# A batched transposed product in float32: the first batch of a loaded ahead of the first pair of b, and the last wait moved from SyncE to GpSimd

## Chip, cores, metric

One core of one Trainium2 chip. The metric is the time of one execution in device microseconds, as a median of several runs. The span that a profile gives for the same execution is some 1.8 us shorter.

## The reference

```python
batch, m, k, n = 16, 512, 512, 512
a: float32 [batch, k, m];  b: float32 [batch, n, k]

def reference(a, b):
    return np.matmul(a.transpose(0, 2, 1), b.transpose(0, 2, 1)).astype(np.float32)
```

Each batch reads 1 MB of a and 1 MB of b and writes 1 MB: 50.33 MB in all.

## The kernel before

The kernel turns all of b before its products, so b's path is long: load, cast to bfloat16 (VectorE), transpose (TensorE), copy out of PSUM (VectorE), product. The path of a is load, cast (ScalarE), product. Batches of b come in pairs of 2 MB, in rows of 16 KB per partition; batches of a in transfers of 1 MB with rows of 8 KB. There are 4 buffers for a, 3 for pairs of b, 5 for pairs of outputs. SyncE issues all loads and the last stores, ScalarE the first five stores.

```python
def run_sp(sp):
    for i in range(B):
        for p in ([0] if i == 0 else [(i + 1) // 2] if i % 2 and i + 1 < B else []):
            if p >= PAIRS:
                sp.wait_ge(turned, p - PAIRS + 1)
            sp.dma_start(b_sb[p % PAIRS][:], b_v[p]).then_inc(b_in[p % PAIRS], 16)
        s, use = i % LOADS, i // LOADS
        if use:
            sp.wait_ge(summed, MO * (i - LOADS) + 1)
        if i % 2 == 0 and i // 2 >= OUTS:
            sp.wait_ge(o_out[i // 2 % OUTS], 16 * (i // 2 // OUTS))
        sp.dma_start(a_sb[s][:], a_v[i]).then_inc(a_in[s], 16)
    # ... stores of pairs 5 and 6 ...
    sp.wait_ge(summed, MO * (B - 1) + 1)
    sp.wait_ge(half_go, 1)
    store(sp, H - 1, slice(0, 1))        # last pair, first batch
    sp.wait_ge(last_go, 3)
    store(sp, H - 1, slice(1, 2))        # the last store
    sp.reg_mov(all_stored, 16 * STORED)

def run_act(act):
    cast_a(act, 0)
    for i in range(B - 1):
        cast_a(act, i + 1)
        copy_out(act, i, slice(2, 4), oa_go)
        # ... store of a pair, three batches behind ...
    act.drain().then_inc(half_go, 1)
    copy_out(act, B - 1, 2, last_go)
    copy_out(act, B - 1, 3, last_go)

# ... casts, copies and turns on VectorE, products on TensorE ...

nc.sync.wait_ge(stored, nc.sync.snap(all_stored))    # behind the section
```

Of the kernel before, what the change touches and what calls it, by code (L numbers as in the profile page):

```python
# [11 lines left out]
def kernel(  # L12
# [6 lines left out]
    nc = tc.nc  # L19
# [15 lines left out]
    a_v = a.rearrange("b (ki ko) m -> b ki ko m", ko=KO)  # L35
# [9 lines left out]
    STORED = H - (H - OUTS) + 1  # L45

    stored = tc.alloc_semaphore("stored")

    all_stored = nc.sync.alloc_register("all_stored")

    with tc.tile_critical():  # L51
        sb = lambda name, shape, dt: ctx.enter_context(nc.sbuf_tensor(name, shape, dt))
# [2 lines left out]
        a_sb = [sb(f"a_sb{s}", [P, KO, M], f32) for s in range(LOADS)]  # L55
# [12 lines left out]
        a_in = [sem(f"a_in{s}") for s in range(LOADS)]  # L68
# [14 lines left out]
        def store(eng, j, part=slice(0, 2)):  # L83

            eng.dma_start(
                out_v[2 * j + part.start:2 * j + part.stop].rearrange("b p mo n -> p b mo n"),
                o_sb[j % OUTS][:, part],
            ).then_inc(o_out[j % OUTS] if j + OUTS < H else stored, 16)

        def run_sp(sp):
            for i in range(B):

                for p in ([0] if i == 0 else [(i + 1) // 2] if i % 2 and i + 1 < B else []):
                    if p >= PAIRS:
# [5 lines that stand above are left out]
                if i % 2 == 0 and i // 2 >= OUTS:  # L101

                    sp.wait_ge(o_out[i // 2 % OUTS], 16 * (i // 2 // OUTS))
                sp.dma_start(a_sb[s][:], a_v[i]).then_inc(a_in[s], 16)

            for j in range(H - TAIL, H - 1):
                sp.wait_ge(summed, MO * (2 * j + 2) + 3)
                store(sp, j)

            sp.wait_ge(summed, MO * (B - 1) + 1)  # L110
            sp.wait_ge(half_go, 1)
            store(sp, H - 1, slice(0, 1))
            sp.wait_ge(last_go, 3)
            store(sp, H - 1, slice(1, 2))
            sp.reg_mov(all_stored, 16 * STORED)

        def run_pool(pool):
            pool.sem_inc(od_go, 1)
            pool.sem_inc(oa_go, 1)
            pool.memset(identity[:], 0.0).then_inc(id_go, 1)  # L120
            pool.wait_ge(id_go, 1)
            pool.affine_select(  # L122
                out=identity[:],
                in_=identity[:],
                compare_op=mybir.AluOpType.not_equal,
                fill=1.0,
                base=0,
                pattern=[[-1, P]],
                channel_multiplier=1,
            ).then_inc(id_go, 1)  # L130

        def cast_a(act, i):
            s = i % LOADS
            act.wait_ge(a_in[s], 16 * (i // LOADS + 1))
            act.copy(a_bf[i % 2][:], a_sb[s][:]).then_inc(ac_go, 1)  # L135
# [56 lines left out]
        def run_pe(pe):  # L192
# [41 lines left out]
            with pe.Fori(0, H) as _i:  # L234
# [6 lines left out]
                half(1, 1)  # L241

        run_sp(nc.sync)
        run_pool(nc.gpsimd)
        run_dve(nc.vector)
        run_act(nc.scalar)
        run_pe(nc.tensor)

    nc.sync.wait_ge(stored, nc.sync.snap(all_stored))  # L250

# [28 lines left out]
```

## Time and profile before

| | before |
|---|---|
| time | 124.8 us (124.68 to 124.91, 3 runs) |
| span | 123.0 us |
| bytes, mean rate | 50.33 MB, 409 GB/s |
| busiest compute engine | PE, 70% of the span |

The page's rows are the span in 40 slices, each digit a busy share in tenths. A stretch is read as: from:to, length, busy time of PE, PEld, DVE, ACT and POOL with counts, granted TensorE clock, DMA share, GB/s (PE is TensorE, PEld its weight loads, DVE VectorE, ACT ScalarE, POOL GpSimd, SP SyncE; a q behind the name is the engine's queue of instructions). A DMA share of 1 means that all 16 DMA engines have a packet in hand. "Landing" is when all of a transfer's semaphore counts have arrived. The lines themselves are in the prediction.

### The profile page before, as it was taken

To read this page: it belongs to the slowest core of one execution; us is meant where nothing else is said; L and a number is where in the kernel's file an instruction comes from. 1 tells how busy PE (TensorE), PEld (TensorE's weight loads), DVE (VectorE), ACT (ScalarE), POOL (GpSimd) and SP (SyncE) were. 2 spreads that over 40 slices of the span, in tenths; PEclk is the share of its full clock that TensorE was granted. 3 is DMA by queue.
4 is the path that set the end of the run, shared out by engine and by line. 5 is a ranking of instruction groups with operands and counts; after the bars stand their busy time and mean duration, and the time that the engine had idled before them with its cause. 6 is when DMAs were issued, how large, how long until landed. Compare 5 with 4: busy or idle time off the path is not lost. (4 is left out here: it accounts for less than half of the span.)

```text
span 123.0 us, 1086 instructions
## 1 busy us (share of the span) xinstructions
PE 86.1 (70%) x400; PEld 49.7 (40%) x400; DVE 56.4 (46%) x48; ACT 46.8 (38%) x34; POOL 0.7 (1%) x6
## 2 busy tenths in 40 slices
PE   0006497997999799779930799965992679979600
PEld 0006344642755464346410546442640526437300
DVE  0016368478295755917039107780719306171200
ACT  4003209537717903176300950329230490750300
POOL 2000000000000000000000000000000000000000
PEclk9999999999999999999995557999999558999995
DMA  4999999999999999999999999999999999999992
GB/s 91 394 400 458 400 424 456 429 394 456 426 397 448 434 376 432 426 440 440 416 421 429 458 408 418 429 426 437 453 397 432 426 426 426 429 426 426 429 424 115
DMA packets 5648, 50.33 MB, mean 409 GB/s; under 512 B 528, under 2 KB 528, under 8 KB 528
## 3 DMA queue, kind: packets, MB, share of 16 engines
q1 hardware_dynamic: 4288, 39.85, 77.2%
q10 hardware_dynamic: 1360, 10.49, 20.1%
HBM read 33.55 MB, written 16.78 MB: 409 GB/s over the span
## 5 line engine op out<-in xcount | busy, mean ns | idle before, releaser
L219 PE MATMUL o_ps<-bt_sb,a_bf 128*128 128x512 bf16 x256 | 65.1, 403 | 7.1 <-PEq L194 6.6
L135 ACT CAST a_bf<-a_sb 128x2048 bf16<-128x2048 f32 x16 | 30.4, 1900 | 40.8 <-DMA a_sb<-in_a_dram 40.8
L219 PEld LDWEIGHTS o_ps<-bt_sb,a_bf 128*128 128x128 bf16 x256 | 28.5, 115 | 37.5 <-issue 15.0
L205 PE MATMUL bt_ps<-identity,b_bf 128*128 128x128 f32 x144 | 24.3, 323 | 22.7 <-PEq L194 22.7
L144 DVE COPY o_sb<-o_ps 128x1024 f32<-128x1024 f32 x16 | 19.6, 1224 | 35.8 <-PE o_ps L219 35.8
L205 PEld LDWEIGHTS bt_ps<-identity,b_bf 128*128 128x128 f32 x144 | 22.2, 212 | 28.2 <-issue 27.2
L152 DVE CAST b_bf<-b_sb 128x2048 bf16<-128x2048 f32 x16 | 19.5, 1221 | 19.1 <-DMA b_sb<-in_b_dram 19.1
L144 ACT COPY o_sb<-o_ps 128x1024 f32<-128x1024 f32 (+1 forms) x17 | 16.4, 962 | 28.0 <-PE o_ps L219 28.0
L161 DVE COPY bt_sb<-bt_ps 128x1024 f32<-128x1024 f32 x16 | 19.5, 1216 | 3.1 <-PE bt_ps L205 3.1
L135 ACT ACT_TABLE_LOAD x1 | 1.3, 1283 | 0.9 <-SPq L51 0.9
L122 POOL TENSOR_SCALAR_AFFINE_SELECT identity<-identity 128x128 f32<-128x128 f32 x1 | 0.3, 294 | 0.2 <-POOL identity L120 0.2
L120 POOL MEMSET identity<- 128x128 f32 x1 | 0.2, 205 | 0.7 <-SPq L51 0.7
L265 POOL MEMSET const-bfloat16-1.0<- 128x1 bf16 x1 | 0.1, 102 | 0.0
L265 POOL MEMSET const-uint8-127<- 128x1 uint8 x1 | 0.1, 102 | 0.0
L265 POOL MEMSET const-float32-0.0<- 128x1 f32 x1 | 0.1, 99 | 0.2 <-issue 0.2
L265 POOL MEMSET const-float32-1.0<- 128x1 f32 x1 | 0.1, 99 | 0.0
## 6 DMA issues: line engine op xcount, KB each, us to landing
b_sb<-in_b_dram SPq DMA_DIRECT2D x8, 2048.0 KB, 20.4
a_sb<-in_a_dram SPq DMA_DIRECT2D x16, 1024.0 KB, 17.5
out_dram<-o_sb ACTq DMA_DIRECT2D x5, 2048.0 KB, 15.2
out_dram<-o_sb SPq DMA_DIRECT2D x2, 2048.0 KB, 13.6
out_dram<-o_sb SPq DMA_DIRECT2D x2, 1024.0 KB, 6.3
```

What stands on the lines that cost most here:

```text
L120: pool.memset(identity[:], 0.0).then_inc(id_go, 1)
L122: pool.affine_select(out=identity[:], in_=identity[:], compare_op=mybir.AluOpType.not_equal, fill=1.0, base=0, pattern=[[-1, P]], channel_ ...
L135: act.copy(a_bf[i % 2][:], a_sb[s][:]).then_inc(ac_go, 1)
L144: copy(o_sb[i // 2 % OUTS][:, i % 2, rm, :], o_ps[h][:, p, :]).then_inc(go, 1)
L152: dve.tensor_copy(b_bf[:, r, :], b_sb[p % PAIRS][:, r, :]).then_inc(bc_go, n)
L161: dve.tensor_copy(bt_sb[g][:].rearrange("p j (ni r) -> p j ni r", r=NR), bt_ps[:].rearrange("p j r (g ni) -> p g j ni r", g=2)[:, g],).the ...
L205: last = pe.transpose(bt_ps[:, j, r, :], w[:, r, j, :], identity[:])
L219: last = pe.matmul(o_ps[h][:, q, :], a_r[:, rk, 2 * h + q, :], bt_h[:, rk // 2, rk % 2, :], start=(rk == 0), stop=(rk == KO - 1),)
L265: nc = _bacc.Bacc("TRN2", target_bir_lowering=False, num_devices=1)
```

## The change

```diff
-    all_stored = nc.sync.alloc_register("all_stored")
+    all_stored = nc.gpsimd.alloc_register("all_stored")
@@ run_sp
             for i in range(B):
+                if i == 0:
+                    sp.dma_start(a_sb[0][:], a_v[0]).then_inc(a_in[0], 16)
@@
-                sp.dma_start(a_sb[s][:], a_v[i]).then_inc(a_in[s], 16)
+                if i:
+                    sp.dma_start(a_sb[s][:], a_v[i]).then_inc(a_in[s], 16)
@@
             store(sp, H - 1, slice(1, 2))
-            sp.reg_mov(all_stored, 16 * STORED)
@@ run_pool
+            pool.reg_mov(all_stored, 16 * STORED)
@@
-    nc.sync.wait_ge(stored, nc.sync.snap(all_stored))
+    nc.gpsimd.wait_ge(stored, nc.gpsimd.snap(all_stored))
```

## The prediction

> **What bounds the kernel now.** I began with the head of the page and its 40 slices, because a kernel of 16 matrix products can be bound by TensorE or by its traffic.
>
> ```profile
> span 123.0 us, 1086 instructions
> PE 86.1 (70%) x400; PEld 49.7 (40%) x400; DVE 56.4 (46%) x48; ACT 46.8 (38%) x34; POOL 0.7 (1%) x6
> ...
> PE   0006497997999799779930799965992679979600
> ...
> DMA  4999999999999999999999999999999999999992
> ...
> HBM read 33.55 MB, written 16.78 MB: 409 GB/s over the span
> ```
>
> The PE row has holes throughout; the DMA row has none between its first slice and its last. No compute engine is over 70% of the span. Next I cut the span into stretches, to see at which rate the transfers run and where they do not (columns: stretch, its length, busy time of PE, PEld, DVE, ACT and POOL with counts, granted TensorE clock, DMA share, GB/s).
>
> ```profile
> 2.00:3.00 1.00, 0.00 (x0) 0.00 (x0) 0.00 (x0) 0.18 (x1) 0.00 (x0) 1.00 1.06 213
> 3.00:4.00 1.00, 0.00 (x0) 0.00 (x0) 0.00 (x0) 0.00 (x0) 0.00 (x0) 1.00 0.71 262
> ...
> 30.00:60.00 30.00, 26.37 (x134) 15.57 (x135) 17.91 (x16) 15.60 (x12) 0.00 (x0) 1.00 1.01 425
> 60.00:90.00 30.00, 21.86 (x96) 12.18 (x93) 14.15 (x12) 10.96 (x8) 0.00 (x0) 0.83 1.01 430
> ...
> 120.00:121.00 1.00, 0.00 (x0) 0.00 (x0) 0.00 (x0) 0.00 (x0) 0.00 (x0) 0.50 0.70 295
> 121.00:122.00 1.00, 0.00 (x0) 0.00 (x0) 0.00 (x0) 0.00 (x0) 0.00 (x0) 0.50 0.04 16
> ```
>
> From 4 to about 120.5 us the rate stays near 427 GB/s, also where TensorE's clock is cut (mean 0.83 between 60 and 90 us). 50.33 MB at 427 GB/s are 117.9 us. The span is therefore: about 1.95 us until the first data packet starts, 1.2 us lost while the rate climbs (20 us into the span 7.18 MB have landed, which at full rate take 16.8 us, so the full-rate line starts at 3.2 us), 117.9 us of transfer, and the rest behind the last data. The chain of waits of the page covers only 5% of the span and stops at ScalarE's last copy, since the last transfer is not an instruction; I did not use it. SyncE's own waits and the issues show how deep the queue is:
>
> ```profile
> SPq L104 <- PE o_ps L219: 41.6, 10, 11.9
> SPq L103 <- DMA out_dram<-o_sb: 33.3, 3, 11.5
> ...
> SPq L276 <- DMA out_dram<-o_sb: 4.6, 1, 4.6
> ```
>
> SyncE waits for buffers for most of the run, yet the DMA engines do not go idle: the loads it has issued are far ahead. The loads' times from issue to landing show by how much:
>
> ```profile
> b_sb<-in_b_dram SPq DMA_DIRECT2D x8, 2048.0 KB, 20.4
> a_sb<-in_a_dram SPq DMA_DIRECT2D x16, 1024.0 KB, 17.5
> ```
>
> A 1 MB load takes 2.45 us at 427 GB/s; a median of 17.5 us means some 15 us of other transfers ahead of it. Over the whole run, behind the first two issues, the shortest is 13.7 us (the load of a issued at 27.2 us). So a stall of SyncE of under about 11 us would not show in the time.
>
> [...] the rate does not change when ScalarE's stores begin at 40 us. [...] The trace agrees for SyncE's first seven loads, which land in the order of issue at 8.8 (b), 11.2 (a), 16.1 (b), 18.6 (a), 21.1 (a), 26.0 (b) and 28.5 us (a). [...] the trace's semaphore records at the end step at 40 to 120 ns, which is the scale that the second part of the change can move.
>
> **The change part by part.** No byte is added or removed, and no compute instruction: VectorE, ScalarE and TensorE have the same instructions in the same order, SyncE one register move less, GpSimd one more. SyncE's first three issues become a, b, b instead of b, a, b; the fourth on is as before.
>
> Part one, start of the transfers. SyncE's first issue still starts at 0.95 us. The first packets start about 1.0 us after it, and take 0.7 to 1.9 us each instead of the 0.61 us that a 16 KB packet takes later. The ramp costs 1.2 us. With a first, the first packets are of 8 KB. If the slow phase is one of time, nothing changes; if each engine pays a delay on its first packet whatever its size, still nothing changes, since the delay is paid once. If it blocks two packets each instead of one, half a packet per engine is lost, 0.3 us. I take +0.05 us.
>
> Part one, compute. b's first pair lands 2.45 us later (8.8 to about 11.2 us), a's first batch earlier (11.2 to about 6.3). Before, b lands at 8.8 us, VectorE casts it in two halves (1.22 us each), TensorE transposes until 13.8, VectorE copies 1.23 us, and the first product starts at 15.55 us. ScalarE's cast of a, begun at 11.25 us and 1.90 us long, is over at 13.15, 2.4 us before it is needed. So the part hurries what had slack, and delays what had none: the first product starts at about 15.55 + 2.45 = 18.0 us. The following waits fold that in. The second pair of b still lands at 16.1 us, and after it VectorE's first gap before a load is only 0.39 us (at 26.0 us), so the lag persists there; but ScalarE waits 3.55 us for a load at 51.7 us and 8.16 us at 67.8 us, so it is gone by the middle. The loads waiting for a buffer are issued 2.45 us later at 16.7 and 17.0 us, in front of which 11.8 us of transfers are still queued (the last landing is 28.5). Nothing runs dry: 0 us.
>
> Part two, the end. The last store is issued at 116.54 us, its last packet ends at 121.45, its semaphore is full at 121.93. SyncE's branch goes at 121.95 to 121.98, SyncE drains at 122.11, reports at 122.17, GpSimd collects at 122.20, and two rounds of the closing barrier end at 122.985. With GpSimd waiting itself, SyncE has reported long before, at about 117.4; what goes is the hop from SyncE to GpSimd, while GpSimd's own branch, drain (34 ns against 7 ns) and collect remain. That leaves at most 122.20 - 122.17 plus a little, which I call 0.05 us; GpSimd might take it back with a slower branch. I take -0.05 us.
>
> Sum: +0.05 + 0 - 0.05 = 0, so 124.8 us.
>
> **The rivals.** First: the late start of compute reaches the end. For it speaks that the last store has little slack: the previous one's data end about 0.5 us before its landing at 119.5, so at 119.0; with 1.0 us from issue to first packet, the store issued at 116.54 may slip 119.0 - 1.0 - 116.5 = 1.5 us before the DMA engines idle. If the whole 2.45 us arrived there, the kernel would take about 1 us more, 125.8. Against it speak the waits for loads named above, of up to 9.1 us, in which the lag disappears, and that later stores let the loads of the same stretch land sooner.
>
> Second: the early a lets compute begin sooner and the tail shrink. It would need the product to wait for a; it waits for b. Even then the transfers, 117.9 us, hold the end: 124.8.
>
> Third: the small first packets shorten or lengthen the ramp, at most the 1.2 us that it costs; half of it would give 124.2 or 125.4. The records of the first packets speak for neither.
>
> Fourth: the new order shifts TensorE's idle stretches and with them the phases at half clock (64.8 to 75.0 and 95.5 to 102.4 us of the span before). One that falls later into the tail could delay the last products by a microsecond or two, of which 1.5 us are free; 125.3 at worst.
>
> **Range and chances.** The three runs of before span 124.68 to 124.91, so 0.1 us of scatter each way. On it come the ramp (0.3 us either way) and the tail (up to 0.5 us, upward only). I predict 124.8 us and a range of 124.3 to 125.3. 2% is 2.5 us: downward, ramp and tail end together hold less than that (1.2 and about 1.5 us, most of which is a barrier that stays), so 0.01; upward it needs a compute lag of over 4 us at the end, 0.03. Within 2%: 0.96.
>
> **What would show it.** The DMA row should again have no hole; the stretches between 30 and 90 us should read 420 to 430 GB/s. The first a should land near 6.4 us, the first b near 11.2, the next five loads as before within 0.3 us. The first product should start near 18.0 us. SyncE should no longer have a long wait for the last store, and from the last landing to the end of the span there should be 0.95 to 1.1 us (before: 1.05). It would be wrong if the rate of the first 6 us differs clearly, if the DMA share falls below 1.0 between the last stores, or if the span behind the last landing grows by more than 0.3 us.

Four passages are cut from the prediction, at the marks, because they say more than the traces and runs show. None of them is a term of the sum: it came to +0.05 + 0 - 0.05 = 0 us, and all its terms stand. One of them argued that no rate is left to gain; that isn't shown, and the forecast takes the flat 427 GB/s as it was measured. Where it says that the trace agrees, the landings behind it are measured. The rate is 431 GB/s from 10 to 30 us, with loads alone, and 431 from 48 to 60 us, with ScalarE's first two stores among the loads (between 46 and 47 us 22 packets of loads start and 29 of a store). The semaphore records at the end are those of 122.18, 122.23, 122.31 and 122.42 us. That later stores let loads land sooner was seen in the changed kernel: its first store moves data from 47.6 us on instead of 44.0, and the eighth and ninth loads of a land at 47.80 and 52.52 us instead of 51.66 and 55.96, though issued 3.5 us later. The fourth rival's "a microsecond or two" is an estimate: with weight loads 0.43 us apart, as in the half clock phase of the profile before, instead of 0.23, the last 8 products would take 1.6 us longer.

## The result

The changed kernel takes 124.67 us (124.49 to 124.74, 6 runs), the kernel before in the same rounds 124.82 (124.6 to 125.45, 6 runs). The ratio is 0.998, with a 95% interval of 0.9957 to 1.0003. A ratio here is the mean time of one kernel's runs over that of the other's of the same rounds, so it isn't quite the ratio of the medians quoted. Executions over 1.5% slower than the fastest of the same kernel are left out of the means. The time is the same within 2%, and a gain of 0.15 us is just not clear of noise.

The page of the changed kernel, its first line and its DMA row:

```profile
span 122.9 us, 1078 instructions
...
DMA  2999999999999999999999999999999999999992
```

The row again has no hole. Its stretches, those that were shown of the kernel before:

```profile
2.00:3.00 1.00, 0.00 (x0) 0.00 (x0) 0.00 (x0) 0.19 (x1) 0.00 (x0) 1.00 0.31 106
3.00:4.00 1.00, 0.00 (x0) 0.00 (x0) 0.00 (x0) 0.00 (x0) 0.00 (x0) 1.00 1.07 451
...
30.00:60.00 30.00, 27.03 (x136) 15.98 (x138) 19.34 (x18) 16.41 (x12) 0.00 (x0) 1.00 1.00 420
60.00:90.00 30.00, 22.02 (x93) 12.33 (x94) 13.88 (x13) 11.36 (x8) 0.00 (x0) 0.83 1.01 431
...
120.00:121.00 1.00, 0.00 (x0) 0.00 (x0) 0.00 (x0) 0.00 (x0) 0.00 (x0) 0.50 0.61 254
121.00:122.00 1.00, 0.00 (x0) 0.00 (x0) 0.00 (x0) 0.00 (x0) 0.00 (x0) 0.50 0.02 8
```

The climb of the rate looks different: slower between 2 and 3 us (106 GB/s, 213 before), but at full rate between 3 and 4 us (451 against 262). (A packet is counted in the stretch in which it starts.) Adding up the bytes of the packet records, the changed kernel is 0.30 us of full-rate transfer ahead from 8 to 41 us. The loads land at 5.7 (a), 10.6 (b), 15.5 (b) and 27.9 us (the fourth of a). From the third on they are 0.6 us earlier than before, more than the lead in bytes, because a landing waits for the last of the 16 DMA engines: the second pair's 16 counts arrive over 1.1 us before and over 0.3 us after. Later 0.2 us of the lead are lost in one place. The stretch from 44 to 48 us, before and after:

```profile
44.00:48.00 4.00, 3.92 (x22) 2.35 (x21) 3.49 (x3) 0.88 (x1) 0.00 (x0) 1.00 1.00 410
```

```profile
44.00:48.00 4.00, 3.23 (x20) 2.43 (x21) 1.79 (x3) 2.75 (x2) 0.00 (x0) 1.00 0.95 371
```

Here some packets of loads take up to 1.13 us before (16 KB, usually 0.611 us) and up to 0.71 us after (8 KB, usually 0.309 us) around the time when ScalarE's first store begins to move data, at 44.0 us before and 47.6 us after. Added up over the DMA engines and divided by 16, this costs 0.14 us before and 0.31 us after. In the changed kernel most of them come ahead of the store's first packet, from 46.6 us on, the store being issued at 43.95 us; so it isn't the stored data that slow them. Behind it the changed kernel leads by 0.11 us, up to the end.

The lead in bytes doesn't set the span alone: the kernel ends when the last of the 16 DMA engines does. By the packet records, that one ends 0.58 us behind the mean of the 16 before and 0.59 us in the changed kernel, so here the 0.11 us reach the end; other kernels differ (below).

SyncE's own waits, and the issues:

```profile
SPq L108 <- PE o_ps L223: 42.8, 7, 14.8
SPq L106 <- DMA out_dram<-o_sb: 32.1, 3, 13.3
```

```profile
a_sb<-in_a_dram SPq DMA_DIRECT2D x16, 1024.0 KB, 14.9
b_sb<-in_b_dram SPq DMA_DIRECT2D x8, 2048.0 KB, 16.0
```

SyncE's wait for the last stores (4.6 us before, named by the transfer it waited for) is gone. The loads are now issued less far ahead: medians of 14.9 and 16.0 us from issue to landing, against 17.5 and 20.4, since compute runs later and frees its buffers later. Part of that is the clock of this one execution (next paragraph): the kernel with the wait alone, with b first, has 16.6 and 19.1. The queue is still deep enough.

The first products, before and after (start, duration, idle time before in brackets):

```profile
15.55 3.80 PE L219 MATMUL o_ps<-bt_sb,a_bf 128*128 128x512 bf16 x16 [1.76 <-PEq L194]
```

```profile
17.43 5.65 PE L223 MATMUL o_ps<-bt_sb,a_bf 128*128 128x512 bf16 x16 [1.76 <-PEq L198]
```

They start 1.9 us later and take 1.85 us longer: the weight loads among them are 0.43 us apart (0.23 before) until about 21.4 us, where the trace's first clock record, of full clock, begins. The page's clock row showed full clock there, because there is no record ahead of it. The spacing is that of half clock: from 99.9 to 101.6 us of the profile before, within a record of clock 0.50 (95.5 to 102.4 us), the weight loads of the same products are 0.43 us apart too. What sets the clock of the first product isn't shown. So compute is 3.5 us late at ScalarE's first store (issued at 43.95 instead of 40.47 us), 2.8 us at the second (54.47, 51.69), and no longer at the third (65.07, 67.85) and fourth (82.16, 82.30).

But the longer first product isn't an effect of the change. Of the 13 profiles with products, nine begin at half clock by this spacing, four of them with b first. The kernel with the wait alone, which loads as before:

```profile
15.53 5.43 PE L219 MATMUL o_ps<-bt_sb,a_bf 128*128 128x512 bf16 x16 [1.76 <-PEq L194]
```

Compared at the same clock, the change puts the first store off by 1.9 us (43.95 against 42.05 us with the wait alone, both at half clock) or 2.0 us (42.45 us with b's bytes in a's place against 40.47 before, both at full clock). The other 1.5 us are the clock of one execution (43.95 against 42.45 us, the two with 1 MB ahead of b).

At the end, the last store is issued at 114.73 us instead of 116.54 and waits its turn: it lands at 121.83 us instead of 121.93. The earlier issue isn't shown to come from the change: with the order alone it is at 116.45 us, with the wait alone at 117.16. From the landing to the end of the span it is 1.03 us instead of 1.05.

### The profile page after: what moved, and what is told of

Read it like the earlier page. It is cut to its first block, busy times and chain, and to the rows that moved or that the text cites. A ratio compares the mean times of both kernels' runs of the same rounds, so it can differ in the third digit from the quotient of the medians.

```text
span 122.9 us, 1078 instructions
## 1 busy us (share of the span) xinstructions
PE 85.1 (69%) x392; PEld 49.4 (40%) x400; DVE 56.2 (46%) x48; ACT 46.8 (38%) x34; POOL 0.7 (1%) x6
## 5 line engine op out<-in xcount | busy, mean ns | idle before, releaser
L223 PE MATMUL o_ps<-bt_sb,a_bf 128*128 128x512 bf16 x248 | 63.6, 405 | 5.8 <-PEq L198 4.8
L209 PE MATMUL bt_ps<-identity,b_bf 128*128 128x128 f32 x144 | 23.7, 317 | 23.2 <-PEq L198 23.2
L209 PEld LDWEIGHTS bt_ps<-identity,b_bf 128*128 128x128 f32 x144 | 21.6, 211 | 28.4 <-issue 27.4
## 6 DMA issues: line engine op xcount, KB each, us to landing
a_sb<-in_a_dram SPq DMA_DIRECT2D x16, 1024.0 KB, 14.9
```

Of the source, the lines that this page charges most:

```text
L209: last = pe.transpose(bt_ps[:, j, r, :], w[:, r, j, :], identity[:])
L223: last = pe.matmul(o_ps[h][:, q, :], a_r[:, rk, 2 * h + q, :], bt_h[:, rk // 2, rk % 2, :], start=(rk == 0), stop=(rk == KO - 1),)
```

## The experiments

Twelve kernels ran, all against the kernel before on the same chip. In the first four's rounds one run of the kernel before took 214.8 us and isn't used. The table gives, from one profile each, by how much the transfers lead those of the profile of the kernel before, in us of full-rate transfer (difference of the bytes moved over 427 GB/s). The span needn't follow it, since the last DMA engine ends it.

| kernel | first transfer | lead at 20 us | at 60 us | at 119 us |
|---|---|---|---|---|
| wait only | b, 16 KB rows | -0.03 | +0.04 | +0.03 |
| tail, one copy | b, 16 KB rows | -0.03 | 0.00 | -0.61 |
| tail, three copies | b, 16 KB rows | 0.00 | +0.06 | -0.58 |
| b in half rows | b, 8 KB at 16 KB pitch | +0.04 | -0.05 | -0.06 |
| changed kernel | a, 8 KB rows | +0.29 | +0.11 | +0.11 |
| order only | a, 8 KB rows | +0.28 | -0.09 | -0.09 |
| transfers only | a, 8 KB rows | +0.28 | -0.12 | -0.03 |
| b 7 us later | a, 8 KB rows | +0.28 | -4.04 | -4.32 |
| b 5 us later | a, 8 KB rows | +0.32 | -0.27 | -0.55 |
| b's bytes in a's place | b, 8 KB rows | +0.20 | +0.01 | +0.01 |
| a in half rows | a, 4 KB at 8 KB pitch | -0.23 | -0.40 | -0.40 |
| a on two queues | a, 8 KB rows | +0.19 | +0.21 | -0.37 |
| b in half partitions | b, 16 KB rows, 64 partitions | -4.53 | -4.47 | -4.45 |

### Order only

The changed kernel with SyncE's wait put back.

```diff
-            pool.reg_mov(all_stored, 16 * STORED)
+            sp.reg_mov(all_stored, 16 * STORED)       # behind the last store, as before
-    nc.gpsimd.wait_ge(stored, nc.gpsimd.snap(all_stored))
+    nc.sync.wait_ge(stored, nc.sync.snap(all_stored))
```

> Only the new order of the first loads; SyncE still makes the last wait. Theory (the transfers set the time, the order gains 0.3 us in the climb of the rate, which the profile of the changed kernel showed as a constant lead of 0.3 us from 5 to 44 us): between 0.1 and 0.4 us under the kernel before, so 124.4 to 124.7 us, first a landing at 5.6 to 5.9 us and the second pair of b at 15.4 to 15.7 (before: 16.1); from the last landing to the end of the span 1.05 us as before. Rival (the climb of that one profile was chance and the 0.15 us come from the wait): no difference from before within 0.1 us, and the second pair of b at 15.4 to 16.2 us at random.

Measured: 124.69 us (124.48 to 124.89, 6 runs), before 124.98; ratio 0.9979, interval 0.9961 to 0.9996. The second pair of b lands at 15.64 us. Its stretch from 3 to 4 us:

```profile
3.00:4.00 1.00, 0.00 (x0) 0.00 (x0) 0.00 (x0) 0.00 (x0) 0.00 (x0) 1.00 1.01 426
```

Full rate there again, so the faster climb is not chance, and the order alone has the gain of the whole change. In this profile the slow packets at the first store cost 0.50 us and the lead ended at -0.09 us. The span is still 0.10 us shorter than before, because the last DMA engine ends only 0.38 us behind the mean of the 16. So the order carries the gain; that the climb carries it to the end is not shown.

### Wait only

The kernel before with GpSimd's wait, and b first.

> Only the wait moved to GpSimd; the first load is b's pair as before. Theory: from the last landing to the end of the span 1.03 us instead of 1.05, so the time is that of before within 0.1 us, with the second pair of b landing at 15.9 to 16.3 us. Rival (the wait carries the gain): 0.1 us or more under before, without any earlier landing.

```diff
-            sp.reg_mov(all_stored, 16 * STORED)
+            pool.reg_mov(all_stored, 16 * STORED)
-    nc.sync.wait_ge(stored, nc.sync.snap(all_stored))
+    nc.gpsimd.wait_ge(stored, nc.gpsimd.snap(all_stored))
```

Measured: 124.82 us (124.65 to 125.23, 6 runs), before 124.98; ratio 0.9994, interval 0.9973 to 1.0014. The second pair of b lands at 16.08 us, and from the last landing (122.08) to the end of the span (123.115) it is 1.03 us. The wait is worth 0.02 us in the profile, and nothing that the runs can show.

### The first pair of b in half rows

```diff
-                    sp.dma_start(b_sb[p % PAIRS][:], b_v[p]).then_inc(b_in[p % PAIRS], 16)
+                    if p == 0:
+                        for r in (slice(0, NR // 2), slice(NR // 2, NR)):
+                            sp.dma_start(b_sb[0][:, r], b_v[0][:, r]).then_inc(b_in[0], 16)
+                    else:
+                        sp.dma_start(b_sb[p % PAIRS][:], b_v[p]).then_inc(b_in[p % PAIRS], 16)
```

(and the wait for this buffer counts 16 more)

> The kernel before, with its first pair of b loaded by two transfers of 1 MB whose rows are 8 KB instead of one of 2 MB with rows of 16 KB; order and waits as before. Theory A (the size of the first packets sets what the climb costs): the second pair of b lands at 15.4 to 15.8 us, as in the changed kernel, and the time falls by 0.1 to 0.4 us. Theory B (it matters that a comes first, or it is chance): it lands at 15.9 to 16.4 us and the time is that of before.

Measured: 125.11 us (124.84 to 125.35, 6 runs); ratio 1.0011, interval 0.9992 to 1.003. The second pair of b lands at 15.98 us, and from 3 to 4 us the rate is that of the other kernels with b first, or little more:

```profile
3.00:4.00 1.00, 0.00 (x0) 0.00 (x0) 0.00 (x0) 0.00 (x0) 0.00 (x0) 1.00 0.84 295
```

The size of the packets alone doesn't make the climb shorter.

### Transfers only

All casts, products and copies are taken out. Loads wait only for the landing of the load before in their buffer, ScalarE's stores for a load three batches on. SyncE's last four stores wait for nothing but the cleared buffers, and are issued at 86 to 89 us instead of 94 to 115. The sizes and the order of the loads are those of the changed kernel.

> Wrong on purpose: no cast, product or copy; the same loads and stores with the changed order, loads waiting only for the landing of the load before in their buffer, stores of zeros behind the landing of the load that is three batches on. Theory (the transfers are the bound and the overlap is complete): 124.3 to 124.8 us, no more than 0.3 us under the changed kernel. Rival (compute holds part of the time, by its late start or its tail): 123.5 us or less.

```diff
-                        sp.wait_ge(turned, p - PAIRS + 1)
+                        sp.wait_ge(b_in[p % PAIRS], 16 * (p // PAIRS))
-                    sp.wait_ge(summed, MO * (i - LOADS) + 1)
+                    sp.wait_ge(a_in[s], 16 * use)
@@ run_dve, run_pe, casts and copies: taken out; output buffers set to 0 once
```

Measured: 124.49 us (124.33 to 124.67, 6 runs); ratio to before 0.9964, interval 0.9947 to 0.9981. Against the order-only kernel of the same rounds this is 0.9964 / 0.9979 = 0.9985, or 0.2 us, with about as much uncertainty either way by the scatter of the six runs of each.

```profile
90.00:116.00 26.00, 0.00 (x0) 0.00 (x0) 1.00 1.01 426
116.00:120.00 4.00, 0.00 (x0) 0.00 (x0) 1.00 1.01 428
```

(Only DVE and POOL stand in these lines, as no other engine works.) The rate is that of the kernels that compute. With all compute gone the kernel is still as long, so no arrangement of compute could have gained more than some 0.2 us beside the order. It says what compute can gain, not what a later start can cost; that is tried below, with b 7 and 5 us later.

The slow packets are here too, with no compute at all: 0.56 us of them from 32.7 us on, the first store being issued at 30.45 us and moving its first packet at 34.1.

### The tail put off

The kernel before with one spare copy of 1.9 us on ScalarE ahead of its last copy, and with three.

```diff
             copy_out(act, B - 1, 2, last_go)
+            for spare in (a_bf[0],):              # or (a_bf[0], a_sb[0], a_sb[1])
+                act.copy(spare[:], a_sb[2][:])
             copy_out(act, B - 1, 3, last_go)
```

> The kernel before with one spare ScalarE copy of 1.9 us ahead of its last copy out, so that the last store is issued some 1.6 us later (about 118.1 us into the span instead of 116.5). The prediction gave that store 1.5 us of slack: the time rises by 0 to 0.4 us. Rival (no slack, the end is the compute chain): it rises by 1.6 us.

> The same with three spare copies: the last store goes out some 5.3 us later, near 121.9 us. With 1.5 us of slack the time rises by 3.8 us, to about 128.6; the DMA share has a gap of that length behind 119 us. Without slack it rises by 5.3 us; if the slack is nearer to the 3.5 us that the ScalarE queue's stores take from issue to first packet less, it rises by more than 5 us as well.

Measured with one copy: 125.58 us (125.01 to 125.83, 4 runs), before 124.83; ratio 1.0059, interval 1.0032 to 1.0086. The last store is issued at 118.46 us, 1.92 us later than before, and the span is 123.56 us, 0.58 longer: 1.34 us of slack. With three copies: 128.24 us (126.68 to 128.93, 4 runs; the one at 128.93 is left out of the ratio); ratio 1.0209, interval 1.016 to 1.0257, on the edge of 2% and so unclear. Here the store is issued at 121.63 us, 5.09 later, and the span is 126.54 us, 3.55 longer: 1.54 us of slack. The stretches show the hole:

```profile
116.00:118.00 2.00, 0.01 (x1) 0.00 (x0) 0.00 (x0) 2.00 (x2) 0.00 (x0) 1.00 1.00 422
118.00:119.00 1.00, 0.00 (x0) 0.00 (x0) 0.00 (x0) 1.00 (x1) 0.00 (x0) 1.00 0.24 98
119.00:120.00 1.00, 0.00 (x0) 0.00 (x0) 0.00 (x0) 1.00 (x2) 0.00 (x0) 1.00 0.00 0
...
122.00:123.00 1.00, 0.00 (x0) 0.00 (x0) 0.00 (x0) 0.00 (x0) 0.00 (x0) 0.50 0.62 262
```

The prediction's 1.5 us for the tail holds. The time with one copy rose by more than expected (0.75 against 0 to 0.4 us), partly because the copy put the store off by 1.92 and not by 1.6 us. So the kernel before was near a bound by its tail: some 1.5 us more of compute and the end moves. In the changed kernel's profile the last store is issued 1.8 us earlier, so there is more room, in that run. The slack differs between executions: with three copies it is 4.91 us from the issue of the last store to the end of the span, with no wait for the DMA engines between; by that measure the slack is 1.54 us in the profile before and 1.05 us with the wait alone.

### b 7 us and 5 us later

The changed kernel with all four first batches of a, or three, ahead of the first pair of b.

```diff
                 if i == 0:
-                    sp.dma_start(a_sb[0][:], a_v[0]).then_inc(a_in[0], 16)
+                    for e in range(4):            # or 3
+                        sp.dma_start(a_sb[e][:], a_v[e]).then_inc(a_in[e], 16)
@@
-                if i:
+                if i >= 4:                        # or 3
```

> The changed kernel with all four first batches of a loaded ahead of the first pair of b, so that b lands near 18.0 us and the first product starts near 24.8 us, 7.4 us later than in the changed kernel and 9.2 later than before. Theory (a late start of compute is swallowed while the queued loads last, some 11 us): 124.5 to 125.7 us. Rival (the start of compute reaches the end): 7 us more, about 132 us.

Measured with four: 128.92 us (128.65 to 129.08, 4 runs), before 124.83; ratio 1.0322, interval 1.0305 to 1.0338. My expectation was wrong. The stretches show why:

```profile
28.00:29.00 1.00, 1.00 (x6) 0.45 (x4) 0.62 (x1) 0.00 (x0) 0.00 (x0) 1.00 0.61 139
29.00:30.00 1.00, 1.00 (x6) 0.34 (x3) 1.00 (x2) 0.00 (x0) 0.00 (x0) 1.00 1.04 442
...
38.00:39.00 1.00, 1.00 (x6) 0.51 (x5) 0.09 (x1) 1.00 (x1) 0.00 (x0) 1.00 0.60 172
```

The DMA engines run out of work at 28 and again at 38 us, and each restart begins with slow packets of about 1 us, as at the start of the kernel. The first load that waits for a buffer is issued at 26.80 us (16.66 before) and the queue's last loads have landed by 27.87. From issue to landing it needs 4.8 us with an empty queue: 0.96 us to the first packet, slow first packets, 2.45 us of transfer, and the time from the last packet to the last count (0.33 to 0.37 us for the first two loads of the kernel before and of the changed one). So of its 14.3 us from issue to landing before, only 9.5 were slack, and it was put off by 10.1. The step "under about 11 us" of the prediction took too much of the landing time for slack, and with compute late throughout, the same loss comes back at the next loads.

> The changed kernel with three batches of a ahead of the first pair of b instead of one, so that compute starts 4.9 us later than in the changed kernel. Theory corrected by the run with four (a late start is free as long as the first load that waits for a buffer is issued before the queue runs dry; in the kernel before that load landed 14.3 us after its issue, less 2.45 of its own transfer, 0.5 of the receipt and 1.9 from issue to first packet, so 9.4 us of slack, of which 2.7 + 4.9 = 7.6 are used here): the queue does not run dry, 124.5 to 125.1 us. Rival (every late start beyond that of the change costs in proportion, half of the delay as in the run with four): 1.5 to 2.5 us more, 126.3 to 127.2 us.

Measured with three: 125.94 us median of 6 runs, from 124.97 to 127.35. Two of them, 127.08 and 127.35, are left out of the ratio, 1.0052 (1.0025 to 1.0078). Neither theory is right. The queue did not run dry in the profiled run (125.97 us), but its slow packets came to more than in any kernel above:

```profile
44.00:48.00 4.00, 3.24 (x15) 1.37 (x13) 2.67 (x4) 2.94 (x3) 0.00 (x0) 1.00 0.95 387
48.00:52.00 4.00, 3.88 (x24) 3.09 (x26) 1.78 (x2) 2.09 (x2) 0.00 (x0) 1.00 1.00 367
```

It lost 0.7 us here, with ScalarE's first store starting, and 0.2 us near 74 us. Its last DMA engine also ends 1.4 us behind the mean of the 16 (0.58 us before), so its span is 1.2 us longer with only 0.55 us of lead lost. (The 1.9 us that the expectation calls the time from issue to first packet hold the slow first packets too; the time itself is 0.96 us, as above. Its 0.5 us of the receipt are the 0.48 us from the end of the last store's last packet to its last count in the kernel before; the first loads took 0.33 to 0.37 us.) The slowest runs have no trace, so what they lost isn't known. What this run shows is that the margin wears thin well before the queue runs dry.

### The second batch of a on ScalarE's queue

```diff
-                if i:
+                if i > 1:
@@ run_act
+            act.dma_start(a_sb[1][:], a_v[1]).then_inc(a_in[1], 16)
```

> The changed kernel with the second batch of a loaded from ScalarE's queue at the start, so that this queue has been used before its first store. In both profiles some loads' packets are slow just when the first store's packets begin (43 to 45 us before, 46 to 50 us after, together worth 0.14 and 0.31 us), and never with a later store. Theory A (first use of the queue): no slow packets at the first store, and the lead of the start is kept: 0.1 to 0.3 us under the changed kernel's 124.67. Theory B (the first writes to the output, or first writes at all): slow packets as before, the time is that of the changed kernel within 0.15 us.

Measured: 124.85 us (124.55 to 125.03, 6 runs); ratio to before 0.9999, interval 0.9985 to 1.0012. In its profile no packet is slow while the first store starts, as theory A says, but nine are at 69 us, of up to 1.3 us, worth 0.40 us, between the last packet of the second store (67.3 us) and the first of the third (70.9 us). The expected gain did not come. So it isn't simply the first use of the queue, nor the first writes. The third store was issued at 67.4 us, so these packets too come between a store's issue and its first packet; what sets them off stays open. The edit does a second thing: the first pair of b now lands at 13.32 us, 2.7 us later than in the changed kernel, and the first product starts at 20.14 us.

### The first pair of b in half partitions, a in half rows, b's bytes in a's place

These three ask what makes the climb shorter when a comes first. (Where one load is cut in two, the wait for its buffer counts 16 more.)

```diff
@@ on the kernel before: half partitions
+                        for q in (slice(0, P // 2), slice(P // 2, P)):
+                            sp.dma_start(b_sb[0][q], b_v[0][q]).then_inc(b_in[0], 16)
@@ on the changed kernel: a in half rows
+                    for ko in (slice(0, KO // 2), slice(KO // 2, KO)):
+                        sp.dma_start(a_sb[0][:, ko], a_v[0][:, ko]).then_inc(a_in[0], 16)
@@ on the changed kernel: b's bytes in a's place (first batch wrong on purpose)
-                    sp.dma_start(a_sb[0][:], a_v[0]).then_inc(a_in[0], 16)
+                    sp.dma_start(a_sb[0][:], b[B - 1].rearrange("(p r) k -> p r k", r=KO)).then_inc(a_in[0], 16)
```

> The kernel before, with its first pair of b loaded by two transfers of 64 partitions each, so that the first transfer covers one contiguous MB with rows of 16 KB,[...] and the order is still b first. Theory A (how far apart the first packets lie sets the climb): the second pair of b lands at 15.4 to 15.7 us, the lead over the kernel before is 0.2 to 0.3 us. Theory B (it is the tensor, or the first row size together with something else): it lands at 15.9 to 16.3 us.

Measured: 129.66 us (129.41 to 129.88, 4 runs); ratio 1.0394, interval 1.0379 to 1.0409. The experiment failed for its purpose, and shows something else. From the third to the twelfth microsecond the rate is about half:

```profile
3.00:4.00 1.00, 0.00 (x0) 0.00 (x0) 0.00 (x0) 0.00 (x0) 0.00 (x0) 1.00 1.11 262
4.00:6.00 2.00, 0.00 (x0) 0.00 (x0) 0.00 (x0) 0.00 (x0) 0.00 (x0) 1.00 1.28 262
```

The DMA share is 1 all the same: the engines have packets in hand that take twice as long (mean 1.20 us instead of 0.61): a mean of 208 GB/s from 3 to 12 us, against 427. What slows the packets of transfers to 64 partitions isn't shown. The 4.5 us lost for 2 MB stay lost to the end, which is another sign that the transfers set the time. The later start of compute isn't the reason: the first product starts at 19.62 us here, and at 20.14 us with a on two queues, which takes 124.85 us.

> The changed kernel, with its first batch of a loaded by two transfers of 512 KB with rows of 4 KB at a pitch of 8 KB. Theory A (pitch of the first packets[...]): the first pair of b lands at 10.6 to 10.8 us as in the changed kernel. Theory C (full contiguous coverage of the first transfer matters): it lands at 10.9 to 11.3 us.

Measured: 125.02 us (124.87 to 125.11, 4 runs); ratio 1.0016, interval 1.0002 to 1.0031. The first pair of b lands at 11.60 us, later than either theory had it: 4 KB rows with holes lose the lead and more.

> Wrong on purpose for the first of the 16 batches: the changed kernel, but the first MB comes from the last batch of b, read as 128 contiguous rows of 8 KB into the buffer of a's first batch. All else, sizes, rows, order and waits, is as in the changed kernel. If the layout of the first transfer (rows of 8 KB that cover one MB without holes) makes the climb shorter, the first pair of b lands at 10.6 to 10.8 us and the time is that of the changed kernel, 124.5 to 124.8 us. If it is the tensor that counts, the first pair of b lands at 10.9 to 11.2 us and the time is that of the kernel before.

Measured: 124.72 us (124.63 to 124.83, 6 runs), before 124.80; ratio 0.9991, interval 0.9972 to 1.001. The first pair of b lands at 10.71 us, within what the layout theory said. From 3 to 4 us:

```profile
3.00:4.00 1.00, 0.00 (x0) 0.00 (x0) 0.00 (x0) 0.00 (x0) 0.00 (x0) 1.00 0.95 401
```

With bytes of b in rows of 8 KB without holes the lead is 0.20 us, two thirds of that with a. So most of the shorter climb comes from the layout of the first transfer, not from the tensor: 8 KB rows that cover one MB gain 0.2 to 0.3 us, the same rows with holes 0.04 us (the other kernels with b first lie between -0.03 and 0), 16 KB rows none, 4 KB rows with holes lose 0.2 us. Each is one profile. Why, these runs don't show; nor whether the remaining third is the tensor or chance.

## Why the prediction was right

- **What bounds the kernel.** Right, and shown: without any compute it takes 124.49 us. One reading was too smooth: ScalarE's first store is issued at 40 us but moves data from 44.0 us on, and there the rate does dip, to 410 GB/s.
- **The compute part.** The first product was put at 18.0 us and came at 17.43; the cost of its delay at 0 us, which holds. The lag was to be gone by 51.7 us or 67.8; at the same clock it was still 1.9 us at the second store (54.47 against 52.58 us) and gone at the third. The 2.8 us seen against the kernel before hold the half clock of one execution. The prediction's waits "named above, of up to 9.1 us" were misread: the 9.1 us are ScalarE's idle time before its first cast at 11.25 us, where no lag can disappear; of those named, 8.16 us is the longest.
- **The climb.** This is the term that was mis-sized, even in its sign: taken as +0.05 us, it was -0.3 us. Landings were missed with it: the first a came at 5.7 us instead of 6.4, the first b at 10.6 instead of 11.2, and the five behind it, which were to stay within 0.3 us, 0.6 us earlier. One of the prediction's own signs of being wrong, a clearly different rate in the first 6 us, came true (259 GB/s, 227 before). The third rival had the right direction, up to -0.6 us, and too much weight on packet size: 8 KB packets alone did not do it. About 0.2 us of the gain were given back with the slow packets at 46 to 50 us, which no step named.
- **The end.** Taken as -0.05 us, it was -0.02 us; moving the wait alone shows no change.
- **The half clock.** The fourth rival's phases did move, to 79.5 to 89.7 us in the changed kernel's profile (a record of clock 0.50), and not into the tail.
- **The sum.** Predicted 0, measured -0.15 us, in the range. The steps' errors were small beside the range, and one of them was paid back by slow packets that nobody foresaw: that the sum came so near 0 is partly luck. That compute could gain no more is not luck; it follows from the transfers. How much of the 0.15 us is the climb's isn't shown, since its lead at the end was +0.11 us in one profile of the new order and -0.09 us in the other.
- **The slack of the tail.** 1.5 us predicted, 1.34 and 1.54 measured by putting it off.
- **The slack of SyncE.** "Under about 11 us would not show" was wrong. At the first waiting load it was 9.5 us, and a start 4.9 us later than the changed kernel's already cost some 0.9 us against it (ratios of 1.0052 and 0.998 to before, of 125 us).

## What to carry to other kernels

When the DMA row has no hole and the rate is flat, take the compute out and time the transfers alone: the difference is about all that any reordering of compute can gain, here 0.2 us of 125 (0.45 with the new order). Slack in a queue is the time from issue to landing less what the transfer itself takes from issue to landing on an empty queue (here 14.3 less 4.8 us), not the whole landing time; and it has to hold at every later load too, if compute stays late (b 7 us later: the queue was empty at 28 us and again at 38). The 2 MB that were cut into two transfers of 64 partitions each cost 4.5 us here; cut into two by rows over all 128 partitions, they cost nothing clear of noise (125.11 us, ratio 1.0011). And a profile is one execution: the clock of the first product, the slow packets and the issue of the last store (114.73 to 117.16 us) differ between kernels that share the code concerned, so a difference of one pair of profiles is looked for in a second pair before it is put down to the change.

## What else the profiles show

- The climb of the rate at the kernel's start: about 1.2 us lost with 16 KB rows first (the kernel before) and 0.9 us with 8 KB rows that cover one MB (the changed kernel; counted in packets that have ended). The first packets take 0.7 to 1.9 us instead of 0.61 before, and 1.03 to 1.16 us for the first six instead of 0.309 after. In the kernel with b 7 us later, whose queue ran dry, it is paid again (packets of about 1 us at 28 and 39 us; 139 and 164 GB/s from 28 to 29 and from 39 to 40 us).
- From the start of SyncE's first issue to its first packet it is 1.0 us (0.95 to 1.96 us in the kernel before), and 0.6 us from the end of that issue. For ScalarE's stores while SyncE's queue is full it is 3.4 to 5.1 us from issue to first packet, before and after the change.
- From the end of the last store's last packet (121.45 us) to its semaphore (121.93) 0.5 us pass in the kernel before, and as long in the changed one (121.35 to 121.83).
- The slow packets of loads in mid run (0.03 to 0.7 us in total near the first store, 0.40 us at 69 us in the kernel with a on two queues), many of them between a store's issue on ScalarE's queue and its first packet. What sets them off is open.
